# Hybrid attention/RWKV layer: small products of the recurrent stage pinned at other places, bonus rows loaded sooner, weight casts queued behind evacuations, and casts and loads at the FFN borders requeued

## The chip, the cores and the metric

The kernel runs on one core of one Trainium2 chip, as one launch. The metric is the device time of that core in microseconds (us): the median of several executions. A profile is one further execution, recorded by the hardware profiler; its span runs from its first to its last instruction.

## The reference

One layer over x of 2048 tokens by 1024 channels, everything float32. Cut to what is computed:

```python
h    = rms_norm(x, pre_mix_g)
proj = h @ w_in                      # 1024 -> 1536 (attention q, k, v) + 1792 (RWKV) + 2048 (gates)
y_a  = chunk_band_attention(q, k, v, rel_bias)   # 8 heads of 64, chunks of 64 tokens, own chunk + 8 before
y_b  = rwkv7_time_mix(p_rwkv, ...)               # token shift, decay, delta-rule state update over time
merged = sigmoid(gate_a) * (y_a @ proj_a) + sigmoid(gate_b) * (y_b @ proj_b)
x    = x + rms_norm(merged @ w_out, post_mix_g)
hf   = rms_norm(x, pre_ffn_g)
u    = jnp.square(jax.nn.relu(hf @ w_up)) @ w_down   # 1024 -> 4096 -> 1024
x    = x + rms_norm(u, post_ffn_g)
```

The end of the RWKV part matters here: the state's output y is normalised in groups of 64 channels, a "bonus" row sum(r * k * r_k) * v is added, and the sum is multiplied by a gate.

## The kernel before

**Number format.** Each float32 operand of a large product is split in two fp32r tiles: a high part, cast by ScalarE (`split`, line 78), and the rest, subtracted by VectorE (line 79). A product is then three matmuls (`mm3`, line 88): high by high, high by low, low by high. The names in the trace are `whi`/`wlo` for weights, `hh`/`hl` for the normalised input.

**Stages.** The tokens are worked in four groups of 512. For each group run in turn `phase_rwkv`, `phase_attention` and `phase_merge` (w_out, and the next group's norm). After the fourth group comes the FFN in two halves, each a `phase_up` and a `phase_down`; both multiply block matrices by a scheme with seven products (`X`, `T`, the names t1 to t4, b22, s1 to s4), with its sums made by VectorE and its operands kept in device memory (`xd`, `wd`, `td`).

**Dense products.** `dense(col)` (line 108) makes 128 columns of h @ w_in for 512 tokens: load of the raw weights by SyncE's (SP's) DMA queue, cast of `whi` by ScalarE and of `wlo` by VectorE, and 24 matmuls of 128x512, first eight hh by `whi`, then eight hl by `whi`, then eight hh by `wlo`. The raw weights, `whi` and `wlo` have two tiles each, and the accumulators (`psd`, pool `pd`) two banks of PSUM. So a dense product can start when the product two before it has been evacuated from its bank, and its `whi` can be cast once the product two before has done its first sixteen matmuls. A group has 14 dense products for the RWKV inputs (`mix`) and 16 for the gates (`gate`) in `phase_rwkv`, 720 matmuls, and 12 in `phase_attention`: q, k, v for each of four head pairs (`att_pair`, line 876). q's evacuation is four ScalarE copies (lines 891, 892) and four VectorE operations (line 894).

**The recurrent stage.** The time recurrence is made of small float32 products on 64x64 and 32x32 tiles. For a pair of head pairs: `rwkv_pre` prepares operands, `rwkv_inverse` solves a triangle step by step on VectorE, `rwkv_blocks` (line 605) has two batches of 32x32 products, `ps_t1` and `ps_t2`, with ScalarE copies between them (`Z`, line 618, and `XT`, line 628), `rwkv_trans` (line 632) transposes (`ps_at`, line 643, in two halves of four) and multiplies, `rwkv_chunk` (line 692) makes the eight steps of the state (`ps_st`, line 699; `ST` on VectorE, line 702), and `rwkv_post` (line 707) normalises (`yn`), transposes back, adds the bonus rows that `rwkv_pre` has stored to device memory (`bvd`, loaded to `bv` at line 736, added at line 737) and multiplies by the gate `ps_g`. `pa`, the PSUM pool of these products, has two banks; the 512-wide temporaries of the stage (`tmp`) have nine tiles.

**What sets the order.** The program is written as Python that records instructions; when it is complete, a planner with its own model of costs orders the queue of every engine: it takes what its model says is ready, the earlier in the program first. Each engine runs its queue in that order and waits with semaphores. Where the planner's model is off, the kernel ties its hands: `queue_behind(ins, first)` makes `ins` stand behind `first` in the queues' order, without a wait of its own; `keep_in_program_order` does what it says; and `place(mm, n)` with `placed()` (line 100) puts a small product behind the dense matmul number n of the group's stage (`self.dl`, counted from 0). `BLOCKS`, `BONUS` and `SCORES` at the top are such numbers: `BLOCKS` = ((412, 424), (623, 632)) puts `ps_t1` and `ps_t2` of the first and the second pair of head pairs behind these dense matmuls.

**The borders.** `branch` (line 1086) multiplies y_a or y_b by a projection and evacuates with one VectorE operation (line 1097). `phase_merge`'s w_out product uses four banks, evacuated after each half by a ScalarE square (line 1136) and a VectorE product (line 1137). `first_half` (line 1218) loads and casts `bh`/`bl`, the operand of the first products of `phase_up`; for the first half of the FFN the planner may put these casts anywhere, for the second they stand behind the weight cast of step 1 of `phase_down`. `phase_up` (line 1229) begins with eight "early" steps, each with one load of w_up, its cast into one of three tiles (a1, s12, s3 in turn), two products and the evacuation `z` (line 1303), and casts the five operands t2, t3, t1, b22, t4 beside them (`operands`). `phase_down` (line 1354) has 56 steps, each with two loads and two casts (`fop`); its `final` loads rows of x1 (line 1430), and `gain` (line 135) loads a row broadcast to all partitions.

Of the kernel before, what the change touches and what calls it, by code (L numbers as in the profile page):

```python
# [35 lines left out]
BLOCKS = ((412, 424), (623, 632))  # L36
# [17 lines left out]
class Block:  # L54
# [52 lines left out]

    def dense(self, col):
# [26 lines left out]
    def gain(self, pool, src, name, bufs=1):  # L135
        t = pool.tile([P, D], F32, tag="gain", bufs=bufs, name=name)
        self.nc.sync.dma_start(t, src[None, :].to_broadcast((P, D)))
        return t
# [217 lines left out]
    def mix(self, g, blk, out):  # L356
# [7 lines left out]
        nc.scalar.activation(out, ps, AF.Copy, scale=self.omu[:, blk : blk + 1])  # L364
# [267 lines left out]
    def rwkv_trans(self, p, R):  # L632
# [7 lines left out]
        for h, cs in enumerate(halves):  # L640
            ps = self.pa.tile([P, 4, P], F32, tag="a", name="ps_at")
            for j in range(4):
                nc.tensor.transpose(ps[:, j], AR[:, h * 4 + j, 0:2].rearrange("p s t -> p (s t)"), self.ident)
# [48 lines left out]
    def rwkv_chunk(self, p, c, R):  # L692
# [5 lines left out]
        for r in rows:  # L698
            nc.tensor.matmul(ps[r], TQ[r, c, 0], S[r], start=True, stop=True)
# [7 lines left out]
    def rwkv_post(self, p, R):  # L707
# [12 lines left out]
        nc.vector.tensor_tensor(yn, Y, rs[:, :, None].to_broadcast((P, NC, C)), ALU.mult)  # L720
        yield
# [13 lines left out]
        bv = self.tmp("bv")  # L735
        nc.sync.dma_start(bv, self.bvd[p])
# [6 lines left out]
    def gate(self, i):  # L743
# [3 lines left out]
        nc.scalar.activation(t, ps, AF.Tanh, scale=0.5, bias=self.hgb[:, i : i + 1])  # L747
# [128 lines left out]
    def att_pair(self, g, p, beside):  # L876
# [12 lines left out]
        for par in range(2):  # L889
            rw, ow = rows[par], rows[1 - par]  # L890
            nc.scalar.activation(QA[rw, par], ps[rw], AF.Copy, scale=-0.125)
            nc.scalar.activation(QB[ow, par], ps[rw], AF.Copy, scale=-0.125)
            for dst in (QB[rw, par], QA[ow, par]):
                nc.vector.scalar_tensor_tensor(  # L894
                    dst, ps[rw], -0.125, QA[rw, par].bitcast(F32), op0=ALU.mult, op1=ALU.subtract
                )
        ps = self.dense(ATT0 + HW + p * P)
        for par in range(2):
            rw, ow = rows[par], rows[1 - par]
            nc.scalar.copy(KK[rw, par, 1], ps[rw])  # L900
            nc.vector.tensor_tensor(KK[ow, par, 1], ps[rw], KK[rw, par, 1].bitcast(F32), ALU.subtract)
        ps = self.dense(ATT0 + 2 * HW + p * P)
        vf = ap.tile([P, G], F32, tag="vf", bufs=1, name="vf")
        nc.scalar.copy(vf, ps)
# [181 lines left out]
    def branch(self, y, br, i):  # L1086
# [10 lines left out]
        nc.vector.scalar_tensor_tensor(t, t, 1.0, ps, op0=ALU.add, op1=ALU.mult)  # L1097
        return t

    def phase_merge(self, g, o, op, between, beside):  # L1100

        tc, nc, a = self.tc, self.nc, self.a
        with ExitStack() as ctx:
# [6 lines left out]
            for i in range(KB):  # L1110
# [4 lines left out]
                self.split(mh[:, i], ml[:, i], t)  # L1115
            self.yctx.close()
            for n in range(2):
# [16 lines left out]
                for t in range(GT):  # L1134
                    sq = op.tile([P, 512], F32, tag="sqo", bufs=2, name="sqo")
                    nc.scalar.activation(sq, ps[t], AF.Square, accum_out=self.ssq[:, g, t, n : n + 1])
# [441 lines left out]
```

## Time and profile before

| | |
|---|---|
| time, median of 3 runs | 3269.18 us (3267.48 to 3270.03) |
| profiled execution: its time, its span | 3272.55 us, 3270.8 us |
| TensorE (PE) busy | 3184.3 us, 97% |
| VectorE (DVE) busy | 2239.5 us, 68% |
| ScalarE (ACT) busy | 1576.9 us, 48% |
| GpSimd (POOL) busy | 596.0 us, 18% |
| DMA | 592.54 MB, 181 GB/s over the span |
| chain that ended last | PE 17%, of which ps_dn 9% and ps_u 8%; every other engine 1% or less |

Busy time of PE is modelled with matmuls that overlap, so 97% says that PE hardly ever had nothing to do, not that it ran at its peak. A wait in the tables is written "who <- whom: us in total, times, longest"; in a timeline the bracket at the end of a row gives the idle time of the engine before the row, and what ended it. PEclk is the share of TensorE's clock that was granted.

### The profile page before, as it was taken

How to read it: one execution, taken by the hardware profiler on the slowest of the kernel's cores; microseconds unless marked ns; L12 is line 12 of the kernel's file. 1: busy time of each engine (PE TensorE's matmuls, PEld its weight loads, DVE VectorE, ACT ScalarE, POOL GpSimd, SP SyncE). 2: the span in 40 equal slices, each digit the busy share in tenths (PEclk: the TensorE clock that was granted, in tenths of full speed). 3: DMA queues.
4: the chain of work that ended last, by engine and by line, in shares of the span. 5: the costliest groups of instructions: out<-in, count | busy, mean ns of one | idle time of the engine just before them, and what ended most of it. 6: DMA issues, size and time to landing. Idle time of an engine off the chain costs nothing. (4 is left out here: it accounts for less than half of the span.)

```text
span 3270.8 us, 50026 instructions
## 1 busy us (share of the span) xinstructions
PE 3184.3 (97%) x18913; PEld 2599.2 (79%) x18913; DVE 2239.5 (68%) x3655; ACT 1576.9 (48%) x2511; POOL 596.0 (18%) x1101
## 2 busy tenths in 40 slices
PE   8999999999999999999999999999999999999998
PEld 6777778777888777878877887888888878888887
DVE  7785666776776785776866775887656768775464
ACT  5434635445745434755434653544543444544343
POOL 2221012122112222112222110122211212120000
PEclk9999999999999999999999999999999999999999
DMA  5245373246574236565336547654777875456565
GB/s 167 85 135 172 126 241 119 72 142 235 181 234 133 88 120 234 182 205 170 94 97 206 182 156 238 226 182 166 254 278 248 290 238 193 167 177 229 193 217 175
DMA packets 432282, 592.54 MB, mean 181 GB/s; under 512 B 25300, under 2 KB 295840, under 8 KB 432040
## 3 DMA queue, kind: packets, MB, share of 16 engines
q1 hardware_dynamic: 373928, 408.94, 39.9%
q0 software_dynamic: 48896, 163.61, 13.7%
q10 hardware_dynamic: 9216, 16.78, 1.4%
q8 instruction: 149, 2.44, 0.3%
q14 instruction: 93, 0.76, 0.1%
HBM read 425.37 MB, written 167.01 MB: 181 GB/s over the span
## 5 line engine op out<-in xcount | busy, mean ns | idle before, releaser
L1409 PE MATMUL ps_dn<-fop 128*128 128x512 f32 x2688 | 611.9, 389 | 1.8 <-DVE fop L79 1.7
L1409 PEld LDWEIGHTS ps_dn<-fop 128*128 128x128 f32 x2688 | 504.0, 188 | 107.8 <-DVE fop L79 2.8
L78 ACT CAST whi<-wraw 128x1024 fp32r<-128x1024 f32 x232 | 243.5, 1050 | 392.9 <-PE psd L88 301.1
L88 PE MATMUL psd<-hh,whi 128*128 128x512 f32 x1344 | 370.3, 403 | 10.7 <-DVE QA L894 10.7
L79 DVE TENSOR_TENSOR wlo<-wraw,whi 128x1024 fp32r<-128x1024 f32 x232 | 283.0, 1220 | 133.3 <-ACT whi L78 70.0
L88 PE MATMUL psd<-hl,whi 128*128 128x512 f32 x1344 | 367.2, 401 | 0.0
L88 PE MATMUL psd<-hh,wlo 128*128 128x512 f32 x1344 | 358.4, 398 | 0.0
L88 PEld LDWEIGHTS psd<-hh,whi 128*128 128x128 f32 x1344 | 244.8, 190 | 59.8 <-issue 11.8
L88 PEld LDWEIGHTS psd<-hl,whi 128*128 128x128 f32 x1344 | 249.1, 190 | 49.5
L88 PEld LDWEIGHTS psd<-hh,wlo 128*128 128x128 f32 x1344 | 247.9, 189 | 50.8 <-issue 1.4
L79 DVE TENSOR_TENSOR fop<-xraw,fop 128x1024 fp32r<-128x1024 f32 x112 | 137.0, 1224 | 178.9 <-ACT fop L78 178.7
L78 ACT CAST fop<-xraw 128x1024 fp32r<-128x1024 f32 x112 | 117.8, 1052 | 256.4 <-PE ps_dn L1409 186.3
L1286 POOL DMA_DIRECT2D xd<-X x192 | 104.2, 545 | 384.2 <-ACT X L1283 321.9
L79 DVE TENSOR_TENSOR fop<-wdraw,fop 128x1024 fp32r<-128x1024 f32 x112 | 136.6, 1220 | 19.0 <-ACT fop L78 18.8
L78 ACT CAST fop<-wdraw 128x1024 fp32r<-128x1024 f32 x112 | 117.7, 1051 | 34.8 <-DMA wdraw<-in_w_down_dram 20.0
L947 DVE CUSTOM_DVE_ANT_0 sc<-bias,ps_s 128x640 f32<-128x640 f32 (+4 forms) x128 | 93.8, 732 | 54.2 <-PE ps_pt L958 27.1
L963 DVE TENSOR_TENSOR PTl<-ps_pt,PTh 128x640 fp32r<-128x640 f32 (+4 forms) x128 | 94.5, 738 | 32.7 <-ACT PTh L962 31.2
L78 ACT CAST s12h<-s 128x1024 fp32r<-128x1024 f32 x32 | 33.7, 1053 | 163.0 <-PE ps_u L88 163.0
L88 PE MATMUL ps_p<-yh,whi 128*128 128x512 f32 x256 | 102.6, 405 | 6.0 <-DVE th L1097 5.3
L962 ACT CAST PTh<-ps_pt 128x640 fp32r<-128x640 f32 (+4 forms) x128 | 79.7, 623 | 55.2 <-PE ps_pt L958 54.6
L952 ACT ACTIVATE sc<-sc,mn 128x640 f32<-128x640 f32 (+4 forms) x128 | 97.8, 764 | 17.4 <-DVE mn L947 15.4
L1126 PE MATMUL ps_o<-whi,mh 128*128 128x512 f32 x256 | 101.4, 396 | 1.8 <-DVE o L1137 1.8
(369 smaller groups left out, 6848.9 us busy)
## 6 DMA issues: line engine op xcount, KB each, us to landing
wraw<-in_w_in_dram SPq DMA_DIRECT2D x168, 512.0 KB
xraw<-xd SPq DMA_DIRECT2D x112, 512.0 KB
xd<-X POOLq DMA_DIRECT2D x192, 256.0 KB, 5.2
wraw<-in_w_up_dram SPq DMA_DIRECT2D x80, 512.0 KB
wdraw<-wd SPq DMA_DIRECT2D x64, 512.0 KB
wdraw<-in_w_down_dram SPq DMA_DIRECT2D x48, 512.0 KB
gd<-gate ACTq DMA_DIRECT2D x64, 256.0 KB
wd<-cmb POOLq DMA_DIRECT2D x64, 256.0 KB, 4.3
```

The source lines that it names most:

```text
L78: high = self.high = self.nc.scalar.copy(hi, src)
L79: self.low = self.nc.vector.tensor_tensor(lo, src, hi.bitcast(F32), ALU.subtract).ins
L88: mm.append(nc.tensor.matmul(ps, l, r, start=n == 0, stop=n == last).ins)
L947: nc.vector.tensor_tensor_reduce(sc[:, 0:n], bias[:, s0:640], pss[:, c0 : c0 + n], 1.0, 3.0e38, ALU.add, ALU.min, mn,)
L952: nc.scalar.activation(sc[:, 0:n], sc[:, 0:n], AF.Exp, scale=-1.0, bias=mn, accum_out=sm[:, col : col + 1])
L962: nc.scalar.copy(hv, pst[:, 0:nk])
L963: nc.vector.tensor_tensor(lv, pst[:, 0:nk], hv.bitcast(F32), ALU.subtract)
L1126: nc.tensor.matmul(ps[t], l[:, k, ts], r[:, k % 2], start=k == 0 and j == 0, stop=k == KB - 1 and j == 2)
L1286: nc.gpsimd.dma_start(self.xd[q][i // 2][:, i % 2], src)
L1409: nc.tensor.matmul(ps, o[:, l, k, sl], o[:, r, k], start=start and n == 0, stop=stop and n == end)
```

## The change

In the recurrent stage:

- `BLOCKS` for the second pair becomes (631, 644); two new pins are added: the first transpose of the second half of `ps_at` of head pair 0 behind dense matmul 438, and the fifth state step (c = 4) of head pair 0 behind 494.
- In `rwkv_post` the tile `bv` and its load stand ahead of the `yield`, directly behind `yn`, and not behind the transposes back.
- Every evacuation of a dense product or of a `branch` product is noted in a list `emptied` as (ScalarE instruction or None, VectorE instruction or None). A new method `follow`, called by `dense` and by each weight cast of `branch`, queues the high cast behind the ScalarE evacuation of three entries before and the low one behind the VectorE evacuation of that entry.

At the borders of the FFN:

- The high casts of `first_half` for the first half stand behind the last high cast of the merge (`self.merged`); for the second half behind the weight cast of step 5, not 1, of `phase_down`.
- The cast of w_up of early step 2 of the first half stands behind the evacuation of the first half of the last group's w_out product (`self.banks`).
- The early steps use the tiles a1, s12, s3, a1, s3, s12, s3, a1; the casts of the operands t2 to t4 begin at step 2, two for each step, behind that step's `z`.
- In `phase_down` the loads of x1 rows and of the gain stand behind the weight load of step 5 (`self.late`).

```diff
-BLOCKS = ((412, 424), (623, 632))
+BLOCKS = ((412, 424), (631, 644))
+TURNED = 438
+FIFTH = 494
...
+    def follow(self):
+
+        for ins, done in zip((self.high.ins, self.low), self.emptied[-3] if len(self.emptied) > 2 else ()):
+            if done is not None:
+                self.queue_behind(ins, done.ins)
...
             self.queue_behind(self.low, self.last_low)
+        self.follow()
         ps = self.pd.tile([P, G], F32, tag="d", name="psd")
...
-                nc.tensor.transpose(ps[:, j], AR[:, h * 4 + j, 0:2].rearrange("p s t -> p (s t)"), self.ident)
+                mm = nc.tensor.transpose(ps[:, j], AR[:, h * 4 + j, 0:2].rearrange("p s t -> p (s t)"), self.ident)
+                if p == 0 and h == 1 and j == 0:
+                    self.place(mm, TURNED)
...
-            nc.tensor.matmul(ps[r], TQ[r, c, 0], S[r], start=True, stop=True)
+            mm = nc.tensor.matmul(ps[r], TQ[r, c, 0], S[r], start=True, stop=True)
+            if p == 0 and c == 4 and r.start == 0:
+                self.place(mm, FIFTH)
...
         nc.vector.tensor_tensor(yn, Y, rs[:, :, None].to_broadcast((P, NC, C)), ALU.mult)
+        bv = self.tmp("bv")
+        nc.sync.dma_start(bv, self.bvd[p])
         yield
...
-        bv = self.tmp("bv")
-        nc.sync.dma_start(bv, self.bvd[p])
         self.tc.keep_in_program_order(nc.vector.tensor_tensor(yf, yf, bv, ALU.add))
...
-            nc.scalar.activation(QB[ow, par], ps[rw], AF.Copy, scale=-0.125)
+            act = nc.scalar.activation(QB[ow, par], ps[rw], AF.Copy, scale=-0.125)
             for dst in (QB[rw, par], QA[ow, par]):
-                nc.vector.scalar_tensor_tensor(
+                dve = nc.vector.scalar_tensor_tensor(
                     dst, ps[rw], -0.125, QA[rw, par].bitcast(F32), op0=ALU.mult, op1=ALU.subtract
                 )
+        self.emptied.append((act, dve))
...
             self.bw = self.wsplit(w.rearrange("(k p) n -> p k n", p=P), "w", NP, 2 * P)
+            self.follow()
...
-                self.split(mh[:, i], ml[:, i], t)
+                self.merged = self.split(mh[:, i], ml[:, i], t)
...
+                if n == 0:
+                    self.banks = squares.ins, scaled.ins
...
             high = self.split_here(bh[:, ks], bl[:, ks])
-            if g:
-                self.queue_behind(high, self.second)
+            self.queue_behind(high, self.second if g else self.merged)
...
-                        self.split_here(h[:, ks], l[:, ks])
+                        self.queue_behind(self.split_here(h[:, ks], l[:, ks]), copied)
...
-                A11, A12 = parts(load(2 * i), ("a1", "s12", "s3")[i % 3], KB)
-                nc.scalar.copy(z[:, i], product(A11, B11, self.pd, "d"))
+                A11, A12 = parts(load(2 * i), ("a1", "s12", "s3", "a1", "s3", "s12", "s3", "a1")[i], KB)
+                if half == 0 and i == 2:
+                    for ins, done in zip((self.cast, self.low), self.banks):
+                        self.queue_behind(ins, done)
+                copied = nc.scalar.copy(z[:, i], product(A11, B11, self.pd, "d")).ins
                 first(i, z[:, i])
-                advance(ops, 1 + i % 2)
+                if i > 1:
+                    advance(ops, 2)
...
+                    if s == 5:
+                        self.late = load.ins
...
                 if s == 1:
                     self.queue_behind(self.relu, high)
+                if s == 5:
                     self.second = high
...
-                nc.sync.dma_start(x, self.x1[g][ts])
+                self.queue_behind(nc.sync.dma_start(x, self.x1[g][ts]).ins, self.late)
...
                     gt = self.gain(op, a["post_ffn_g"], "g_post2")
+                    self.queue_behind(self.gained, self.late)
```

The other notes of an evacuation (in `mix`, `gate`, k and v of `att_pair`, `branch`) have the same form as the one shown for q.

More of the change, by code (lines that the diff above doesn't have):

```diff
@@ L136, in gain @@
         t = pool.tile([P, D], F32, tag="gain", bufs=bufs, name=name)
-        self.nc.sync.dma_start(t, src[None, :].to_broadcast((P, D)))
+        self.gained = self.nc.sync.dma_start(t, src[None, :].to_broadcast((P, D))).ins
         return t
@@ L363, in mix @@
         nc.gpsimd.tensor_copy(self.carry[:, blk : blk + 1], pr[:, G : G + 1])
-        nc.scalar.activation(out, ps, AF.Copy, scale=self.omu[:, blk : blk + 1])
+        self.emptied.append((nc.scalar.activation(out, ps, AF.Copy, scale=self.omu[:, blk : blk + 1]), None))
         nc.vector.scalar_tensor_tensor(
@@ L746, in gate @@
         t = self.sp.tile([P, G], F32, tag="gate", bufs=2, name="gate")
-        nc.scalar.activation(t, ps, AF.Tanh, scale=0.5, bias=self.hgb[:, i : i + 1])
+        self.emptied.append((nc.scalar.activation(t, ps, AF.Tanh, scale=0.5, bias=self.hgb[:, i : i + 1]), None))
         nc.scalar.dma_start(self.gd[i], t)
@@ L1389, in operands @@
                 else:
-                    nc.sync.dma_start(wr, wrows[w[0]][:, 2 * f : 2 * f + 2, w[1]])
+                    load = nc.sync.dma_start(wr, wrows[w[0]][:, 2 * f : 2 * f + 2, w[1]])
+                    if s == 5:
+                        self.late = load.ins
                 self.split(t[:, 0], t[:, 1], xr)
@@ L1485, in run @@
             consts = self.constants(ctx, mixing)
+            self.emptied = []
             advance(consts, 1)
```

13 lines of the change are left out of this document (7 added, 6 removed).

## The prediction

> **What bounds the kernel now.** I read the page first, then the clock, then PE's waits, then the timeline around each long wait.
>
> ```profile
> PE 3184.3 (97%) x18913; PEld 2599.2 (79%) x18913; DVE 2239.5 (68%) x3655; ACT 1576.9 (48%) x2511; POOL 596.0 (18%) x1101
> core 0: 3270.8 us, clock 0.993
> 3262.00:3270.80 8.80, 0.00 (x0) 0.00 (x0) 4.04 (x6) 0.65 (x3) 3.12 (x6) 0.63 0.64 229
> ```
>
> PE is the bound: what it computes stays, so the change can only win time in which PE stands still, or in which its clock is low. The clock's mean of 0.993 over 3270.8 us means 0.007 x 3270.8 = 22.9 us lost. The third row, a window behind the last matmul with a granted clock of 0.63, holds 0.37 x 8.8 = 3.3 us of that, so 19.6 us lie where PE works. PE's waits are these, who waited for whom, total, times, longest:
>
> ```profile
> PE psd L88 <- DVE QA L894: 10.7, 4, 2.9
> PE ps_at L643 <- ACT XT L628: 9.4, 4, 2.4
> PE ps_t L615 <- DVE X L593: 6.8, 5, 1.7
> PE ps_p L88 <- DVE th L1097: 5.3, 5, 2.5
> PE ps_st L699 <- DVE ST L702: 5.1, 4, 1.3
> PE ps_t L623 <- ACT Z L618: 4.7, 8, 0.8
> PE ps_u L88 <- ACT z L1303: 2.3, 3, 1.5
> PE ps_u L88 <- ACT s12h L78: 1.8, 2, 0.9
> PE ps_o L1126 <- DVE o L1137: 1.8, 1, 1.8
> PE ps_dn L1409 <- DVE fop L79: 1.7, 3, 0.8
> PE ps_g L88 <- DVE yn L720: 1.5, 4, 0.4
> ```
>
> Five of them come four times (once a group, `ps_t` L623 twice), so they are built into the order of the queues. The clock follows them. Windows of 4 us behind such waits, with PE's instructions in the third column and the granted clock third from the end:
>
> ```profile
> 143.10:147.10 4.00, 3.89 (x40) 2.79 (x40) 0.16 (x1) 2.19 (x6) 0.00 (x0) 0.69 0.23 67
> 1131.70:1135.70 4.00, 3.89 (x60) 3.12 (x62) 1.13 (x1) 2.57 (x6) 0.43 (x1) 1.00 0.21 63
> 305.85:309.85 4.00, 4.00 (x10) 3.13 (x11) 1.26 (x2) 0.58 (x1) 0.70 (x1) 0.50 0.53 169
> 788.00:792.00 4.00, 4.00 (x18) 3.29 (x19) 2.53 (x3) 1.73 (x3) 1.56 (x4) 1.00 1.15 328
> 2004.40:2008.40 4.00, 4.00 (x11) 3.16 (x12) 2.86 (x4) 1.26 (x3) 0.00 (x0) 0.57 1.09 318
> ```
>
> The first two stand behind the same wait (`ps_at`) in groups 0 and 2: with the clock at 0.69 PE gets through 40 instructions, at 1.00 through 60. The next two stand behind q's evacuation: 10 against 18. Going through the span so I count eleven stretches of low clock before the last matmul, the first at 143.10 and the last at 2004.40, each behind one of the listed waits: three at `ps_at`, four at the second pair's `ps_t`, a double one at q in group 0, one each at `ps_p` and `ps_o`.
>
> **Part 1, the three pins.** Positions are counts of dense matmuls, in group 0, between the waits:
>
> ```profile
> 19.10:143.05 123.95, 104.18 (x429) 80.31 (x429) 0.00 (x0) 17.63 (x29) 1.00 0.44 125
> 143.05:192.50 49.45, 17.91 (x60) 10.97 (x60) 0.00 (x0) 3.13 (x5) 0.97 0.16 51
> 192.50:236.70 44.20, 33.02 (x135) 24.88 (x135) 0.00 (x0) 3.43 (x5) 1.00 0.56 174
> 236.70:241.00 4.30, 2.34 (x9) 1.61 (x9) 0.00 (x0) 0.68 (x1) 1.00 0.45 120
> ```
>
> So 429 stand ahead of the waiting `ps_at`, 489 ahead of the waiting `ps_st`, 624 and 633 ahead of the second pair's two batches. Behind number 438, 494, 631 and 644 they will be 439, 495, 632 and 645: 10, 6, 8 and 12 more. A dense matmul costs 0.227 us, by the first two rows here:
>
> ```profile
> 231.39 1.98 PE L88 MATMUL psd<-hl,whi 128*128 128x512 f32 x8
> 233.20 1.98 PE L88 MATMUL psd<-hh,wlo 128*128 128x512 f32 x8
> 236.83 1.20 PE L615 MATMUL ps_t<-X,NA 32*32 32x32 f32 x64 [1.65 <-DVE X L593]
> 241.11 0.24 PE L623 MATMUL ps_t<-XT,Z 32*32 32x32 f32 x2 [0.82 <-ACT Z L618]
> 227.96 1.06 ACT L78 CAST whi<-wraw 128x1024 fp32r<-128x1024 f32 x1 [1.61 <-PE psd L88]
> 229.78 0.69 ACT L747 ACTIVATE gate<-psd,hgb 128x512 f32<-128x512 f32 x1 [0.76 <-PE psd L88]
> 241.09 0.58 ACT L618 COPY Z<-ps_t 32x512 f32<-32x512 f32 x1
> 235.72 1.06 DVE L593 STREAM_TRANSPOSE X<-X 128x512 f32<-128x512 f32 x1
> ```
>
> Second pair: dense product 26 (matmuls 624 to 647) has its `whi` at 229.02 and its bank at 230.47, so 8 of its matmuls can fill from 235.0, where product 25 ends (233.20 and 8 x 0.227), to 236.8, where `X` is ready (236.78). The first batch starts where it did. The copies `Z` end at 241.67 either way, and 13 matmuls behind the batch's end at about 238.0 reach 240.9. So 12 x 0.227 = 2.7 us of dense work go where PE waited 1.65 + 0.82 + 0.36, at no delay: 10.9 us in four groups.
>
> `ps_at`: the 10 are 429 to 438, three of product 17 and seven of product 18.
>
> ```profile
> 140.37 0.69 ACT L364 ACTIVATE r<-psd,omu 128x512 f32<-128x512 f32 x1
> 141.88 1.16 ACT L628 COPY XT<-ps_t 32x512 f32<-32x512 f32 x2
> 143.10 0.66 PE L643 MATMUL ps_at<-ident,AR 128*128 128x128 f32 x4 [2.35 <-ACT XT L628]
> ```
>
> The bank for product 18 is free at 141.06, when the three are being done, and `XT` at 143.04: the ten, 2.27 us, fit into the 2.35, and I take 2.2 each, 8.8 in all. The lower end is the three alone, 0.7 each, if the planner puts the bank's evacuation behind `XT`. `ps_st`: 6 x 0.227 = 1.36 against 1.3, of a product already begun; 5.1 in all. The state steps behind it come 0.1 us later, hidden under the dense stream.
>
> **Part 2, q's evacuation, `follow` and the bonus rows.** v's product waits for q's bank:
>
> ```profile
> 297.05 0.69 DVE L737 TENSOR_TENSOR yf<-yf,bv 128x512 f32<-128x512 f32 x1 [4.01 <-DMA bv<-bvd]
> 303.05 1.22 DVE L79 TENSOR_TENSOR wlo<-wraw,whi 128x1024 fp32r<-128x1024 f32 x1 [2.09 <-ACT whi L78]
> 305.01 0.69 DVE L894 SCALAR_TENSOR_TENSOR QA<-psd,QA 64x512 fp32r<-64x512 f32 x1
> 305.85 3.75 PE L88 MATMUL psd<-hh,whi 128*128 128x512 f32 x8 [2.90 <-DVE QA L894]
> ```
>
> The cast at 303.05 is that of the next pair's q, which cannot start before k's product has ended; q's last two evacuations stand behind it. `follow` puts it, and the high cast on ScalarE, behind them. VectorE was idle from 300.96 (303.05 less 2.09), and the two need 1.4: they end by about 302.4, ahead of the end of k's product (302.95, which is 305.85 less 2.90). Without the 4.01 us on `bv`, which the earlier load takes away, they have 3 us more. All 10.7 us go. Behind the cast that now waits stand only its own product, whose start is later still. `follow` elsewhere orders what was in that order already: nothing. The bonus load passes one or two weight loads in SP's queue, 0.5 us of issue; the raw tiles it delays are ahead by a product (5.4 us), so nothing, if its tile is free (see the rivals).
>
> **Part 3, the FFN borders.** The 2.5 us of `ps_p` are these:
>
> ```profile
> 1968.32 1.23 DVE L1215 TENSOR_TENSOR bl<-bl,bh 128x1024 fp32r<-128x1024 f32 x1 [2.48 <-ACT bh L1214]
> 1970.07 0.68 DVE L1097 SCALAR_TENSOR_TENSOR th<-th,ps_p 128x512 f32<-128x512 f32 x1
> ```
>
> A `first_half` cast, itself waiting, stands ahead of an evacuation; behind the last cast of the merge it can't: 2.5. The cast of step 2 leaves the way of the w_out evacuation: one cast (1.23) of 1.8, so 1.2. The operand casts behind `z`, and the tiles that leave s12 free early, take both `ps_u` waits: 2.3 + 1.8 = 4.1. Step 5 for the second half's casts and the x1 and gain loads: 1.3 of the 1.7 at `ps_dn` (the long two). Sum 9.1; the lower end is 5, if s3, now reused after two steps, waits as long as s12 did, 0.9 at four places.
>
> **The clock.** If the waits go, the low stretches go: 19.6 us at most, none at least. Of 4 us at 0.69, 1.24 us are lost, at 0.50 2.0; I take 1.4 each, since small products and waits take part of the stretch: 15.4. Here a rule speaks against the sum. The Trainium skill, "TensorE: Matmul & The Clock Gate", section "Why this matters for your kernels", warns of PE-idle gaps over about 3 us; by that none of these waits would cost clock, and the sum would be 15.4 us smaller. The trace disagrees: 0.69 behind a wait of 2.35 us.
>
> **The sum.** 10.9 + 8.8 + 5.1 + 10.7 + 9.1 = 44.6 of waits, and 15.4 of clock: 60.0. What is late next? New pins leave short waits where the planner's model is off; the nearest row is `ps_g`'s, 0.37 each, and with four changed places in four groups that is 6; with four reuses of s3 at 0.4, 1.6. So 8 back, 52 net. The profiled execution took 3272.55 us (its span and 1.75 around it), so 3220.5; the median of the runs lies 3.4 below it: **3217 us**.
>
> **Rivals.** *The clock stays low* (0.12): the stretches come from the 32x32 and 64x64 products that stand behind the waits and keep most of the array idle, and they remain. For it: the 2.6 us wait at 788 left the clock at 1.00, and so did the 2.35 in group 2. Against it: the long 512-wide streams at 305.85 and 2004.40 were hit, with no such products near. 60 - 15.4 - 8 = 37: 3232.
>
> *The filler is missing later* (0.17): 28 dense matmuls a group, 6.4 us, are spent early, and PE stands still for them when the last normalisation of the stage is late. For it: `ps_g` waits for `yn` there now. Against it: attention's q and k, 48 matmuls, can fill if the planner's model sees the wait. 52 - 4 x 6.4 = 27: 3242.
>
> *`follow` binds nothing* (0.05): then q's 10.7 and its clock (2.8) stay: 3231. *All of it is moved and comes back elsewhere* (0.04): 3269.
>
> *Slower* (0.04): the bonus load now asks for a temporary while nine are in use, and SP, waiting for it, holds up the weight loads behind. A block of B us costs PE about B - 5.4, at eight places; it passes the 52 at B = 12, and with B = 16.3, three whole products, it gives 87 - 52 = 35 more: 3304. Against it: at `yn` the operands of the pair before have been read, and two posts hold six of nine.
>
> **Numbers.** Forecast 0.58; 0.92 of all cases are faster by over 0.2% (6.5 us, about what a measurement of this kernel can tell from no change), 0.04 the same, 0.04 slower. The low end, 3203, has no short waits (8), the whole clock (4) and the remaining 0.1 to 0.5 us of Part 1's waits (2); the high end, 3247, takes in the missing filler with the lower ends of Part 3 (4).
>
> **What would show it.** Right: the waits of `ps_at`, `ps_st`, `psd` on QA, and both `ps_t` under 1 us in total a group; the mean clock 0.997 or more; no DVE wait on `bv`. Wrong: a wait of PE before `ps_yt` or `ps_g` of several us (filler), SP waiting at the bonus load (slower), low clock without waits (the first rival), or L894 still behind a cast (`follow`).

## The result, and the profile after

The changed kernel takes 3239.04 us (median of four runs, 3238.18 to 3240.22), the kernel before 3269.61 us beside it (3267.48 to 3270.29). The ratio is 0.9909 (95%: 0.9893 to 0.9925): 30.6 us faster, where 52 were forecast. The time lies inside the range, 22 us above the forecast of 3217. One execution of a later run, filled_st, took 6308 us, and all comparisons leave it out.

The page of the profiled execution (3239.38 us) has PE's row and the core's span and clock as follows; before, it was 3184.3 us busy of 3270.8 at a clock of 0.993.

```profile
PE 3171.4 (98%) x18913; PEld 2591.0 (80%) x18913; DVE 2240.1 (69%) x3655; ACT 1577.4 (49%) x2511; POOL 604.5 (19%) x1101
core 0: 3237.7 us, clock 0.997
```

PE's waits in the kernel after: who waited for whom, total, times, longest.

```profile
PE pstr L156 <- DVE xn L360: 11.5, 4, 8.1
PE ps_yt L742 <- ACT yf L747: 9.7, 4, 3.5
PE ps_st L710 <- DVE ST L715: 4.2, 4, 1.1
PE ps_s L956 <- DVE mn L962: 3.9, 5, 1.1
PE ps_o L1142 <- DVE wlo L81: 3.7, 5, 1.6
PE ps_p L90 <- ACT yh L80: 3.4, 4, 1.3
PE ps_p L90 <- DVE th L1113: 2.3, 5, 0.8
PE ps_g L90 <- DVE yn L733: 1.5, 4, 0.4
```

The reader is to see what left the list and what entered it. Gone, or at most 0.9 us, are `psd` on QA, `ps_at`, both `ps_t`, `ps_u` on s12h and z, `ps_dn`. The wait at `ps_st` is still there. And the second row is new: `ps_yt`, four times, once a group, for the activations `yf` that empty its bank. Before, PE did not wait there at all.

The clock was low in three places instead of eleven. These are windows of the kernel after, the granted clock third from the end:

```profile
395.10:398.50 3.40, 3.32 (x10) 2.02 (x8) 1.23 (x4) 0.86 (x3) 0.00 (x0) 0.50 0.23 77
698.90:702.30 3.40, 3.38 (x11) 2.57 (x11) 3.02 (x12) 2.43 (x5) 0.54 (x1) 0.50 0.81 227
1200.60:1204.00 3.40, 3.39 (x12) 2.66 (x13) 3.06 (x11) 2.80 (x6) 0.32 (x1) 0.51 0.73 209
```

The second and the third stand right behind the new wait. In the clock records of these traces every low stretch ahead of the last matmul has a clock of one half and a length of 3.413 us (or twice that), so each 3.413 us costs 1.71 us.

With that, the time of PE can be split. For each profiled execution I took the time from the first matmul to the end of the last, and from it two things: the time in which no matmul ran (from the end of one to the start of the next, put down to the tile of the next), and 1.71 us for each low stretch. What is left is PE's own work. All in us:

```
               before  no_pins  early_only  blocks_only  no_turned  after  after_again  yf_first  yt_pin  filled
ps_at             9.4      9.4         0.3          9.4        9.4    0.2          0.3       0.2     0.3     0.2
ps_t             11.9      9.2         3.5          1.3        7.4    1.2          0.8       5.8     4.8     1.4
ps_st and ps_y    5.1      4.0         4.7          4.0        3.7    4.7          4.7       4.7     4.7     4.6
ps_yt             0.0      1.3         8.7          3.1        0.0    9.8          8.6       0.0     0.8     1.0
these four       26.4     23.9        17.2         17.8       20.5   15.9         14.4      10.7    10.6     7.2
psd (q, k, v)    10.7      0.0         1.1          0.0        0.0    1.1          1.1       1.1     1.1     1.1
ps_p              6.7      3.0         5.7          4.5        5.0    6.4          4.8       7.1     4.5     4.1
ps_s              1.9      4.5         4.5          4.6        4.3    4.3          4.5       6.7     6.2     6.9
ps_u, ps_dn       5.9      2.5         2.2          2.5        1.8    2.0          2.1       2.3     3.8     2.0
no matmul, all   67.3     49.3        47.2         46.7       47.4   47.0         43.0      44.3    42.4    36.9
low clock        18.8     10.2         5.1          6.8        5.1    5.1          3.4       6.8     5.1     0.0
rest           3165.6   3164.2      3165.6       3165.1     3166.8 3166.3       3166.0    3163.6  3165.2  3169.1
```

The last row moves by 5.5 us at most: PE's work is nearly the same in all of them, and most of what sets one kernel apart from another is in the two rows above it. Differences of a few us can't be told from the one profile that each kernel has; that of no_pins is the fastest of its four executions. Numbers at the end of a name are left out in the trace, so the row `ps_s` holds attention's `ps_s` and also `ps_s0`, a product of the recurrent stage behind `ps_t`; the latter waits 2.5 us in yf_first, 1.6 in yt_pin, 2.3 in filled, and not at all in the others. From before to after 20.3 us of standing still and 13.7 us of low clock are gone, 34.0 in all; the profiled executions differ by 33.2. The columns between are the experiments.

### The profile page after: what moved, and what is told of

Same layout as the page of the kernel before. It is cut to its first block, busy times and chain, and to the rows that moved or that the text cites. A ratio compares the mean times of both kernels' runs of the same rounds, so it can differ in the third digit from the quotient of the medians.

```text
span 3237.7 us, 50020 instructions
## 1 busy us (share of the span) xinstructions
PE 3171.4 (98%) x18913; PEld 2591.0 (80%) x18913; DVE 2240.1 (69%) x3655; ACT 1577.4 (49%) x2511; POOL 604.5 (19%) x1101
## 5 line engine op out<-in xcount | busy, mean ns | idle before, releaser
L90 PE MATMUL psd<-hl,whi 128*128 128x512 f32 x1344 | 358.4, 396 | 0.0
L1142 PE MATMUL ps_o<-wlo,mh 128*128 128x512 f32 x256 | 100.4, 392 | 3.7 <-DVE wlo L81 3.7
```

The costliest lines, as they stand in the source:

```text
L90: mm.append(nc.tensor.matmul(ps, l, r, start=n == 0, stop=n == last).ins)
L1142: nc.tensor.matmul(ps[t], l[:, k, ts], r[:, k % 2], start=k == 0 and j == 0, stop=k == KB - 1 and j == 2)
```

## The experiments

The first theory: the waits that the pins remove come back at `ps_yt`. In the kernel after, ScalarE and PE do this in group 1 (timeline; start, duration, engine and line, work, and in brackets the idle time ahead and what ended it):

```profile
689.03 1.05 ACT L80 CAST whi<-wraw 128x1024 fp32r<-128x1024 f32 x1 [0.45 <-DMA wraw<-in_w_in_dram]
695.26 1.05 ACT L80 CAST whi<-wraw 128x1024 fp32r<-128x1024 f32 x1 [5.19 <-DMA wraw<-in_w_in_dram]
696.22 0.68 ACT L760 ACTIVATE gate<-psd,hgb 128x512 f32<-128x512 f32 x1
696.80 0.55 ACT L744 ACTIVATE yf<-ps_yt,cst 64x256 f32<-64x256 f32 x1
697.36 0.56 ACT L747 ACTIVATE yf<-ps_yt,gbo,gwo 64x256 f32<-64x256 f32 x1
```

VectorE ahead of that, and PE:

```profile
687.52 1.21 DVE L81 TENSOR_TENSOR wlo<-wraw,whi 128x1024 fp32r<-128x1024 f32 x1
```

```profile
693.13 1.03 PE L742 MATMUL ps_yt<-ident,yn 128*64 128x128 f32 x8
695.38 0.40 PE L90 MATMUL psd<-hh,whi 128*128 128x512 f32 x1
697.98 0.63 PE L742 MATMUL ps_yt<-ident,yn 128*64 128x128 f32 x4 [2.20 <-ACT yf L747]
```

The first post's `ps_yt` is done at 694.2, and its `yf` could start. But a high cast for a later product is ahead in ScalarE's queue and waits 5.19 us for its weights. Its raw tile became free only when VectorE's `wlo` cast of 687.52 had read it, and the load that was issued behind that landed at 695.2. So `yf` starts at 696.80, and the second post's `ps_yt`, which needs the bank, waits until 697.98. PE could have gone on with its dense product, whose weights are ready, but one matmul only stands ahead of that `ps_yt` in its queue. The rival: the wait has to do with the bonus rows' load, which the change puts ahead of two weight loads in SP's queue.

**no_turned.** The pin of `ps_at` taken out of the kernel after:

```diff
-                if p == 0 and h == 1 and j == 0:
-                    self.place(mm, TURNED)
```

> The kernel after without the pin of ps_at behind dense matmul 438 (TURNED). Theory (given back at ps_yt: the pinned matmuls bring PE to the first post earlier than the weights can be staged): PE's wait for XT at ps_at, 9.4 us in before, returns with up to 3.7 us of low clock, and the wait at ps_yt, 9.7 us in after, falls below 4 us and its two low stretches (3.4 us) go: 3239 + 13.1 - 5.7 - 3.4 = 3243 us (3238 to 3246). Rival (the ps_yt wait has another cause, such as the bonus load that is issued earlier): ps_yt keeps its 9.7 us and the ps_at wait comes on top: 3239 + 13.1 = 3252 us (3248 to 3254).

Measured: 3240.77 us, ratio 0.9931 (0.9914 to 0.9948). PE's waits:

```profile
PE ps_at L652 <- ACT XT L637: 9.4, 4, 2.4
PE ps_t L624 <- DVE X L602: 4.5, 5, 1.0
PE ps_y L712 <- DVE ST L713: 3.7, 4, 0.9
PE ps_t L632 <- ACT Z L627: 2.5, 8, 0.4
```

`ps_yt` is not among them: its 9.7 us are gone to nothing, and `ps_at`'s 9.4 are back. That is the theory, not the rival. But 6.2 us also came back at `ps_t`, which neither had: where PE doesn't wait at `ps_yt`, it is too early for X.

**no_pins.** All three pins as before:

```diff
-                    self.place(mm, TURNED)
...
-                self.place(mm, FIFTH)
...
-BLOCKS = ((412, 424), (631, 644))
+BLOCKS = ((412, 424), (623, 632))
```

> The kernel after with none of the three new pins (no TURNED, no FIFTH, BLOCKS at their old counts); follow, the earlier bonus load and the FFN borders stay. Theory (given back at ps_yt): the waits of before at ps_at (9.4), the second pair's ps_t (about 11) and their low clock (7 stretches, about 10 us) return, the ps_yt wait of 9.7 us and its low clock (3.4) go: 3239 + 30 - 13 = 3256 us (3251 to 3260), and PE's wait at ps_yt is under 2 us. Rival (ps_yt waits because of the earlier bonus load or follow): ps_yt keeps over 7 us, 3239 + 30 = 3269 us (3264 to 3272).

Measured: 3249.35 us, ratio 0.9952 (0.9935 to 0.9968); `ps_yt` waits 1.3 us. So the three pins together are worth 0.9952 less 0.9911 (the mean of after's two ratios), 0.0041 of 3265 us: about 13 us, with some 5 us of doubt on each ratio. The time lies below the theory's range of 3251 to 3260, though the wait at `ps_yt` went as it said. The prediction had 24.8 us for them and some 10 of clock (seven stretches at 1.4).

**old_bonus.** The bonus rows' load back behind the activations:

```diff
-        bv = self.tmp("bv")
-        nc.sync.dma_start(bv, self.bvd[p])
         yield
...
+        bv = self.tmp("bv")
+        nc.sync.dma_start(bv, self.bvd[p])
         self.tc.keep_in_program_order(nc.vector.tensor_tensor(yf, yf, bv, ALU.add))
```

> The kernel after with the bonus rows' load back at its old place behind the yf activations; all else stays. Theory (ps_yt waits because PE comes earlier than the weights): the wait at ps_yt stays over 7 us; VectorE waits for bv again (4.0 us each time), which q's evacuation bears since follow keeps the cast behind it: 3239 us (3236 to 3245). Rival (the bonus load's new place in SP's queue, ahead of two weight loads, delays those weights): the ps_yt wait falls under 3 us with its low clock, 3239 - 6.7 - 3.4 = 3229 us.

Measured: 3238.62 us, ratio 0.9916 (0.9899 to 0.9934), the same as after; `ps_yt` waits 7.0 us. The rival falls. VectorE, in the second pair of posts of group 0 and behind it:

```profile
291.31 0.69 DVE L750 TENSOR_TENSOR yf<-yf,bv 128x512 f32<-128x512 f32 x1 [4.03 <-DMA bv<-bvd]
297.20 0.69 DVE L907 SCALAR_TENSOR_TENSOR QA<-psd,QA 64x512 fp32r<-64x512 f32 x1
297.93 1.23 DVE L81 TENSOR_TENSOR wlo<-wraw,whi 128x1024 fp32r<-128x1024 f32 x1
```

The wait for `bv` is back with its 4.03 us, and it costs PE little (`psd` waits 2.2 us, 1.1 in after): with `follow`, q's last evacuation stands ahead of the cast.

**no_follow.** The other half of that pair, both calls of `follow` out:

```diff
-        self.follow()
         ps = self.pd.tile([P, G], F32, tag="d", name="psd")
...
-            self.follow()
         wh, wl = (x[:, :, i % 2 * P : (i % 2 + 1) * P] for x in self.bw)
```

> The kernel after without follow: the weight casts aren't queued behind the evacuations of three products before; the earlier bonus load, the pins and the FFN borders stay. Theory (the prediction's second part: the cast that stands ahead of q's last two evacuations holds v's product up, and taking VectorE's 4 us on bv away isn't enough): PE's wait for QA returns, 8 to 10.7 us in four groups, with up to two low stretches of 1.7 us: a ratio to before of 0.9945 (0.9935 to 0.9955), some 11 us slower than after. Rival (the earlier bonus load alone frees VectorE in time): the wait for QA stays under 2 us and the ratio is that of after, 0.991.

Measured: 3233.17 us, ratio 0.9911 (0.9897 to 0.9926). The theory's 11 us did not come back; the rival was right. VectorE at the same place:

```profile
298.22 0.69 DVE L906 SCALAR_TENSOR_TENSOR QA<-psd,QA 64x512 fp32r<-64x512 f32 x1
299.13 1.23 DVE L81 TENSOR_TENSOR wlo<-wraw,whi 128x1024 fp32r<-128x1024 f32 x1 [0.22 <-issue]
```

With the bonus rows there in time, the order comes out the same without being asked for. Each of the two edits alone takes most of the 10.7 us away: `psd` waits 2.2 us with `follow` alone, 1.1 with the earlier load alone, 1.1 with both. But `follow` moves other waits. Attention's `ps_s` waits 2.3 us here and 1.9 in before, against 4.3 to 4.7 in the eleven profiles that have `follow`; `ps_p` waits 0.5 for `yh` and 4.7 for `th` here, 3.4 and 2.3 in after.

**yt_pin.** One more pin on the kernel after, so that eleven matmuls fill the wait at `ps_yt`:

```diff
+NORMED = 588
...
+                mm = nc.tensor.transpose(ps[:, j], yn[:, h * 4 + j], self.ident)
+                if p == 1 and h == j == 0:
+                    self.place(mm, NORMED)
```

> The kernel after with one more pin: the first ps_yt transpose of the second post stands behind dense matmul 588, so that eleven matmuls (2.5 us) of a product whose weights are ready fill the time until the yf activations have freed the bank. Theory (given back at ps_yt): the wait at ps_yt falls from 9.7 to under 2 us and the two low stretches behind it (3.4) go; X is ready 1.4, 2.6, 2.7 and 0.9 us ahead of its product in after, so that 0.8, 0, 0.8 and 0.9 us come back at ps_t: 3239 - 8 - 3.4 + 2.5 = 3230 us (3226 to 3233). Rival (PE is ahead of everything that the stage has to give, and any filler spent here is missing at the stage's end): the wait moves to ps_t or to the last ps_yt, 3239 us (3236 to 3242).

Measured: 3233.78 us, ratio 0.9904 (0.9888 to 0.9921), just above the theory's range and not to be told from after by its interval. `ps_yt` fell from 9.8 to 0.8 us; 3.6 came at `ps_t`, and there are three low stretches still, at 387.6, 421.7 and 708.5.

**yf_first.** The same wait taken away from the other side: the cast that waits for its weights is queued behind the last `yf`, and no pin is touched.

```diff
+        if len(self.dl) == 600:
+            self.waiting = self.high.ins
...
+            self.queue_behind(self.waiting, self.released)
```

> The kernel after with one cast moved: the high cast of the 26th dense product, which in after waits some 5 us on its weights' transfer ahead of the first posts' yf activations, is queued on ScalarE behind the last of them; no pin is changed. Theory (ps_yt waits because that cast, waiting for its weights, holds up the yf activations that free the bank): the wait at ps_yt falls from 8.5 to 9.7 us to under 2 us and its low stretches go; as with the pin at 588 part of it comes back at ps_t for X: 3 to 8 us faster than after, a ratio of 0.9885 to 0.990. Rival (the bank comes free late for another reason, such as the gate's evacuation or the activations' own 4.5 us): the wait stays over 6 us and the ratio at 0.991.

Measured: 3234.88 us, ratio 0.9915 (0.990 to 0.993). ScalarE in group 1, and some of PE's waits:

```profile
692.98 0.69 ACT L764 ACTIVATE gate<-psd,hgb 128x512 f32<-128x512 f32 x1 [3.25 <-PE psd L90]
693.56 0.55 ACT L746 ACTIVATE yf<-ps_yt,cst 64x256 f32<-64x256 f32 x1
```

```profile
PE ps_t L626 <- DVE X L604: 5.5, 6, 1.2
PE ps_st L712 <- DVE ST L717: 4.2, 4, 1.1
PE ps_s L697 <- DVE TQ L690: 2.5, 2, 2.0
```

`yf` starts 0.8 us behind `ps_yt`'s start (692.78) instead of 3.7, and `ps_yt` waits 0.0: the cast was the cause of that wait. But the theory's gain did not come. 4.6 us moved to `ps_t`, where PE now waits for X, 2.5 to `ps_s0` (line 697), where it waits for VectorE's `TQ`, and four low stretches remain, one of them behind that last wait. The four places together fell by 4 to 5 us, `ps_s0` took back some half of it, and the ratio is that of after.

These two runs ask what sets X. Counted from each group's first `ps_z`, the second pair's X is ready at 203.6, 204.9, 203.5 and 205.0 us in before, at 201.6, 203.0, 204.1 and 203.1 in after, at 201.4, 202.6, 202.7 and 203.0 in yf_first. It comes about 2 us earlier in three groups of after, where PE comes to the first `ps_yt` 3.4 or 3.5 us earlier, and 0.6 later in the third. So I formed a second theory, the budget: VectorE's chain sets when the stage reaches X, and only the count of dense matmuls ahead of the last pin decides how long PE stands still until there. Rival: the prediction, every pin by itself. The four kernels below ran beside one another.

**after_again.** The kernel after, as a base.

> The kernel after, unchanged, as the base for the three runs beside it: 3239 us if this chip grants the clock as in its first runs, and down to 3234 us where it doesn't (before was 5.7 us faster on the chip of the first experiments). Both theories: a ratio to before of 0.991.

Measured: 3236.64 us (3233.31 to 3241.5), ratio 0.9913 (0.9897 to 0.9929). Its profiled execution had two low stretches instead of three, and 4 us less standing still: so much the same kernel varies in one profile.

**blocks_only.** `TURNED` and `FIFTH` out, `BLOCKS` new.

```diff
-                if p == 0 and h == 1 and j == 0:
-                    self.place(mm, TURNED)
...
-            if p == 0 and c == 4 and r.start == 0:
-                self.place(mm, FIFTH)
```

> The kernel after with, of the three pins, only BLOCKS at its new counts (no TURNED, no FIFTH). New theory (budget: X of the second pair is ready some 203 us behind the group's start whatever PE does, so only the count of dense matmuls ahead of the last pin, 644, decides; the pins ahead of it only say where in that stretch PE waits): within 3 us of after, with ps_at's 9.4 us of wait back, none at ps_yt, and the second batch of ps_t within 1.5 us of its place in after. Rival (the prediction: each pin gives its own sum): 8.8 + 5.1 us of waits and 3 low stretches of 1.7 us come back, 19 us slower than after, or 9 us slower if ps_yt's 9.7 us go.

Measured: 3239.16 us, ratio 0.992 (0.9905 to 0.9934), 2.5 us above after. The two pins that I had priced at 13.9 us are worth 2.5 by these medians when `BLOCKS` is there, as the budget has it. Two of its details are off: `ps_yt` still waits 3.1 us, and the second batch of `ps_t` starts up to 2.3 us away from its place in after, not 1.5.

**early_only.** `TURNED` and `FIFTH` in, `BLOCKS` old.

```diff
-BLOCKS = ((412, 424), (631, 644))
+BLOCKS = ((412, 424), (623, 632))
```

> The kernel after with TURNED and FIFTH but BLOCKS at its old counts. New theory (budget): no better than with no pin at all, since 632 matmuls stand ahead of the second batch of ps_t either way: 9 to 13 us slower than after, the 3.6 us a group that the two pins fill come back as waits at ps_t for X or at ps_yt. Rival (the prediction): the 10.9 us of BLOCKS and its low clock come back but the 13.9 us of the other two pins stay: 13.9 us faster than no_pins, which is within 3 us of after.

Measured: 3238.35 us, ratio 0.9919 (0.9904 to 0.9933), 1.7 us above after. The budget wanted the time of no_pins and is wrong here. The rival's time came, within 3 us of after, but not its way, for the wait at `ps_t` did not come back. PE's waits at the places in question:

```profile
PE ps_yt L742 <- ACT yf L747: 8.6, 4, 3.4
PE ps_st L710 <- DVE ST L715: 4.2, 4, 1.1
PE ps_t L624 <- DVE X L602: 2.7, 4, 0.9
```

As with after, the wait at `ps_at` went to `ps_yt`, but the one at `ps_t` shrank to 3.5 as well, from 9.2 in no_pins. Most of that is the wait for `Z`, 4.7 us there and 0.6 here. ScalarE ahead of it in group 0 of no_pins, then of early_only:

```profile
236.53 1.25 ACT L609 COPY XT<-XD 32x512 f32<-32x512 f32 x2 [6.43 <-DVE XD L604]
237.80 1.05 ACT L80 CAST whi<-wraw 128x1024 fp32r<-128x1024 f32 x1
238.75 0.68 ACT L756 ACTIVATE gate<-psd,hgb 128x512 f32<-128x512 f32 x1
239.46 0.58 ACT L627 COPY Z<-ps_t 32x512 f32<-32x512 f32 x1
```

```profile
233.81 1.06 ACT L80 CAST whi<-wraw 128x1024 fp32r<-128x1024 f32 x1 [2.94 <-PE psd L90]
235.55 1.24 ACT L609 COPY XT<-XD 32x512 f32<-32x512 f32 x2 [0.68 <-DVE XD L604]
236.82 0.69 ACT L760 ACTIVATE gate<-psd,hgb 128x512 f32<-128x512 f32 x1
237.53 0.58 ACT L627 COPY Z<-ps_t 32x512 f32<-32x512 f32 x1
```

In no_pins the cast for a dense product stands between `XT` and `Z`, and `Z` starts 2.9 us behind `XT`; in early_only the planner has put that cast ahead of `XT`, and `Z` starts 2.0 us behind it. It is so in all four groups. The pins on PE's queue have changed the order of ScalarE's, at a place that neither pin names and neither theory counted. So neither theory holds as it stood. What the table shows is that the pins don't add: from no_pins, the first two alone save 6.7 us at the four places, the third alone 6.1, all three 8.0 to 9.5.

**filled.** More matmuls ahead of the last pin, with the wait at `ps_yt` filled:

```diff
-BLOCKS = ((412, 424), (631, 644))
-FIFTH = 494
+BLOCKS = ((412, 424), (640, 653))
+FIFTH = 498
+NORMED = 588
```

> The kernel after with the pin of the second post at 588 as in yt_pin, FIFTH at 498 in place of 494 and BLOCKS at (640, 653) in place of (631, 644): nine more dense matmuls a group, 2.04 us, ahead of the last pin. New theory (budget): PE's waits at ps_st (4.2 us in yt_pin) and ps_t for X (4.5) are filled, 4 x 2.04 = 8.2 us less than yt_pin, about 13 us less than after: 3226 us, with the second ps_t batch at its place of yt_pin within 0.5 us. Rival (filler is missing later): what is spent here is missing at the stage's end, and the time stays that of yt_pin within 2 us, with new waits of PE at the last ps_yt or ps_g of each group.

Measured: 3227.87 us (3225.2 to 3229.93), ratio 0.9885 (0.9869 to 0.9901), 8.8 us below after beside it, with no run of the one among the runs of the other. Its span, clock, and PE's waits in the stage:

```profile
core 0: 3225.2 us, clock 0.999
```

```profile
PE ps_y L715 <- DVE ST L716: 4.2, 4, 1.1
PE ps_s L696 <- DVE TQ L689: 2.3, 3, 0.9
PE ps_g L91 <- DVE yn L734: 1.5, 4, 0.4
PE ps_yt L743 <- ACT yf L750: 1.0, 2, 0.5
```

The four places hold 7.2 us, there is no low stretch before the last matmul, and `ps_g` is where it was: the nine matmuls a group that are spent early are not missing at the stage's end. The row `ps_s` is `ps_s0`, with 2.3 us. The theory's time came nearly, its place did not: the second batch of `ps_t` starts 0.1 to 2.2 us later than in yt_pin, not within 0.5. It beats both kernels.

**filled_st.** filled, with the 4.2 us at `ps_y` attacked: the fifth step's products of both pairs behind 502.

```diff
-            if p == 0 and c == 4 and r.start == 0:
+            if p < 2 and c == 4 and r.start == 0:
...
+                self.place(mm, FIFTH)
```

> The kernel filled of the second experiments with one more change: the fifth step's products of both head pairs, the ps_y ones too, stand behind dense matmul 502 (in filled only the first ps_st stood behind 498, and PE waited 1.05 us a group at ps_y of the same step). Theory (this wait, too, is only a place where VectorE is behind, and dense matmuls that are there fill it): the 4.2 us at ps_st and ps_y go, the others stay, a ratio to before of 0.987 (filled had 0.9885). Rival (VectorE's chain sets the time of the next batches, so the wait moves to ps_t or to another step): 0.9885, with as much more wait elsewhere in the stage.

Measured: 3235.08 to 3238.32 us in three executions, ratio 0.9922 (0.9905 to 0.9938): both theories fail, it loses some 12 us against filled. Why stays open: no profile shows these three executions.

**old_border.** The FFN borders as before, the rest as after:

```diff
-            self.queue_behind(high, self.second if g else self.merged)
+            if g:
+                self.queue_behind(high, self.second)
...
-                        self.queue_behind(self.split_here(h[:, ks], l[:, ks]), copied)
+                        self.split_here(h[:, ks], l[:, ks])
...
-                A11, A12 = parts(load(2 * i), ("a1", "s12", "s3", "a1", "s3", "s12", "s3", "a1")[i], KB)
+                A11, A12 = parts(load(2 * i), ("a1", "s12", "s3")[i % 3], KB)
...
-                self.queue_behind(nc.sync.dma_start(x, self.x1[g][ts]).ins, self.late)
+                nc.sync.dma_start(x, self.x1[g][ts])
```

> The kernel after with the FFN borders' casts, tiles and loads queued as in before (follow's part in the merge stays). Theory (the prediction's third part holds): the waits at ps_p behind the first_half cast, ps_o at the w_out evacuation, ps_u for s12 and z and ps_dn return, about 7.6 us, with one or two low stretches: a ratio to before of 0.9935 (0.9925 to 0.995). Rival (these waits are only moved about): the ratio stays at 0.991, other waits at ps_p, ps_o and ps_u going as these come.

Measured: 3244.31 us, ratio 0.9948 (0.9932 to 0.9965), 0.0037 of 3263 us, or 12 us, above after. The waits of before are back in their places:

```profile
PE ps_p L90 <- DVE th L1113: 4.1, 3, 2.3
PE ps_o L1142 <- DVE o L1153: 2.4, 1, 2.4
PE ps_u L90 <- ACT z L1321: 2.3, 3, 1.7
PE ps_u L90 <- ACT s12h L80: 1.8, 2, 0.9
PE ps_dn L1429 <- DVE fop L81: 1.5, 2, 0.8
```

## Why the prediction was right, and where it was wrong

**q, follow and the bonus rows (10.7 us): right in size.** `psd` waits 1.1 us instead of 10.7. The prediction argued from both edits at once; the runs show that either is enough, so one of them is a safeguard and no gain. That `follow` would be worth nothing elsewhere was wrong: with it, attention's `ps_s` and `ps_p` on `yh` wait longer, `ps_p` on `th` shorter (see no_follow).

**FFN borders (9.1 us): the places right, the size too large.** Without these edits the waits that they aimed at are back. But in after other waits stand in part of their room, `ps_p` on `yh` and `ps_o` on `wlo`: over `ps_p`, `ps_o`, `ps_u` and `ps_dn` PE stands still for 15.9 us in old_border, and for 12.1 and 9.1 in the two profiles of after. That is 4 to 7 us in place of 9.1, with the clock of one or two stretches (1.7 to 3.4) beside it; PE's time from first to last matmul grows by 4 to 10 us. The 12 us by the ratios are more, with some 5 us of doubt on each. Of the two waits at `ps_u` I had them wholly gone; 2.0 us stay there, on VectorE's sum `x` and on z.

**The clock (15.4 us): near, by two errors that offset each other.** 13.7 us came. The forecast had all eleven stretches gone at 1.4 us each; eight went at 1.71, half a clock for 3.413 us. The Trainium skill, "TensorE: Matmul & The Clock Gate", section "What's actually happening", has the activity of PE judged in free-running windows of 3413 ns; the trace agrees, with 3.413 us, and in each trace the stretches begin whole multiples of 3.413 us apart. The rival "the clock stays low" is refuted: eight stretches went with their waits.

**The pins (10.9 + 8.8 + 5.1 us): here it failed.** The step is the addition of these three in "The sum", with 6 us for the short waits that new pins leave. At the three named places 20.3 of the 24.8 us did go (9.2 at `ps_at`, 10.7 at `ps_t`, 0.4 at `ps_st`), but 9.8 came up at `ps_yt`, ahead of the last pin. Three things are wrong with the sum.

First, the counts are cumulative. Ten more matmuls ahead of `ps_at` are the same matmuls as the six (in the trace eight) ahead of `ps_st` and the twelve ahead of the second batch of `ps_t`; at the last pin PE has twelve more behind it, not 28. By twelve, four groups and 0.227 us the three pins are good for 10.9 us, not 24.8. The four places hold 10.5 and 12.0 us less than before in the two profiles of after. Between `ps_at` and the waiting `ps_st` two matmuls fewer stand than before, not more, and that wait (5.1 us) is still 4.7. The count isn't all, as early_only shows: there 4.1 of the 6.7 us that the pins save at the four places come by the order of ScalarE's queue.

Second, I took PE's arrival for the only thing that moves. The weights for the products between don't come earlier when PE does: their raw tiles are freed by casts on VectorE, which is busy there. In group 1 the load that the cast ahead of `yf` waits for goes out 180.9 us behind the first `ps_z` in before and 181.2 in after. So the gained time reappeared at the first place where ScalarE's queue has a cast for such weights ahead of something that PE needs, `ps_yt`. In the trace of after PE reaches the first `ps_yt` 3.5, 3.5, 2.2 and 3.4 us earlier than before (from each group's first `ps_z`, with as many dense matmuls behind it), and the second one, a single matmul on, 1.2, 1.2, -1.4 and 1.4 us earlier. The same cast stood ahead of `yf` in before: `yf` starts at 188.6, 189.8, 188.5 and 190.0 us there, at 188.0, 189.2, 190.4 and 189.1 in after. I had costed the pins against the bank and `XT` at the pin itself, and had not walked on to the next place where PE waits on ScalarE. The rival "the filler is missing later" put the new wait at the stage's last normalisation, with 25.6 us; there it is 0, and 9.8 us are at the first. Its sign, a wait before `ps_yt`, came, but not its cause: filled spends nine more matmuls a group early and is faster. That its 3242 us is near the result is chance.

Third, what fills one wait is missing at another. Waits at `ps_yt`, `ps_st` and `ps_t` take each other's place: without `ps_yt`'s 9.8, `ps_t` has 4.6 more and `ps_s0` 2.5.

**What is late next (8 us): mis-sized.** From before to after, 9.8 us appeared at `ps_yt`, 2.4 at attention's `ps_s`, 3.1 at `ps_p` on the cast `yh` (0.3 to 3.4). With the 4.7 at `ps_st` that never went that is 20.0 in place of 8. That is 12.0 of the 16.3 us by which the standing still fell short of the forecast (44.6 less 8, 36.6, against 20.3).

The rival "slower", the bonus load that blocks SP, showed nothing: old_bonus, without it, is no faster.

**Open.** What moves X by about 2 us between the kernels; why the planner changes ScalarE's order as it does; what ended the gain of filled_st; and what each pin is worth alone, for the differences between after, blocks_only and early_only are smaller than their intervals.

## What to carry to other kernels

A pin moves work from one wait to another, and counts along one queue are cumulative: don't add up pins that are filled by the same matmuls. A planner may also order the other engines' queues anew, as in early_only, so read these again. Look for the next place where the engine that is now earlier meets one that is not. When a wait is filled, see which engine's queue holds a command that waits for a transfer ahead of one that frees a bank. Two edits that cure the same wait are worth one; take each out alone before crediting either.

## What the runs showed of the hardware

Leaving out filled_st, there are thirteen profiles, with 45 low stretches ahead of the last matmul (two of them of double length; filled has none). In the 3.413 us ahead of each, PE had stood still for at least 1.16 us in sum (1.16 to 3.38). The Trainium skill, "TensorE: Matmul & The Clock Gate", section "Why this matters for your kernels", puts the bound at idle gaps of about 3 us; here sums of a third of that were followed by half a clock, among them the two gaps of 0.8 and 0.4 us at the second pair's `ps_t`.

Within a trace, low stretches begin whole multiples of 3.413 us apart. Cut into windows along that grid, from 10 us behind the first matmul on, the twelve traces that have such stretches show what decides. All 22 windows in which PE stood still for 1.95 us or more were followed by a low one. Of the 75 windows with 1.16 to 1.92 us, 23 were, and of the rest none, but for the two that made a stretch double. So the same wait costs clock or none by where it falls on the grid: the 3.14 us in old_bonus fall on two windows, 1.89 and 1.25, of the three waits of 2.61 in before at most 1.70 lies in one window, and none of these was followed by half a clock. Nine of the 23 hold 1.16 to 1.19 us of standing still beside 1.20 to 1.44 us of 32x32 products, which suggests that such products count in part as standing still; no run tests it.

The runs of one kernel differ in clock: after_again took 3233.31 us at a mean clock of 0.998 and 3241.5 at 0.996, and before took from 3258.66 to 3270.29 us over all its runs. So a difference of 5 us needs a base on the same chip, and the table of what PE waited for says more than one time.
